# A decoder step on one core: feed-forward without marking products, the last pair's products apart, the last tile added in its bank, first weights on another queue, a planner with new costs

## The chip, the cores and the metric

The kernel runs on one core of one Trainium2 chip. The core has five engines with a queue of instructions each: PE (matrix products into PSUM, whose 2 KB rows are called banks here), ACT, DVE and POOL (elementwise), and SP, which issues most DMA transfers. ACT and POOL issue some too. The metric is the device time in microseconds (us); lower is better. Times are medians of rounds; one execution is also profiled.

## The reference

One inference step of one decoder layer for a prompt of 512 tokens and a sample group of 8 x 4 tokens, which share all weights; D_MODEL is 1024, D_FF 2816, everything in float32.

```python
h = rmsnorm(x, norm_mix)
z = h @ w_in                       # 8 heads of dilated attention, 4 heads of a gated recurrence (HGRN2)
x = x + concat([att, o]) @ w_out   # both normalised per head
c = rmsnorm(x, norm_cross)         # cross attention over 256 memory rows
x = x + co @ w_co
u = rmsnorm(x, norm_ffn)
ug = u @ w_gate
conv = conv_b + sum(conv_w[j] * up[:, j:j + T] for j in range(CONV_W))   # up: ug behind its state
x = x + (jax.nn.silu(conv) * (u @ w_up)) @ w_down
y = rmsnorm(x, norm_final)
```

Beside y the outputs are the new keys and values, the recurrent states, the memory's keys and values and the last rows ahead of the convolution.

## The kernel before, in words

All 544 tokens lie along the free dimension, features on the 128 partitions: x is 8 tiles of 128 x 544. A product of full precision is made of three passes of a faster type (float32r): each operand is split into a high part (a copy, by ACT) and a low part (a subtraction, by DVE), and high x high, high x low and low x high are added in one PSUM bank (`passes`, line 920). A tile of weights (128 output features, 1024 inputs) is thus 24 products for each of two cuts of the tokens: `CUTS`, 256 and 288 columns, or `HALVES`-like cuts of 272.

*Pairs.* Most of the feed-forward takes two tiles of weights together with Strassen's scheme (Winograd's form): seven block products in place of eight, each of 12 passes with 272 columns (`Pair`, line 2356). The seven are numbered as in the code: 1 is A11 x B11, 2 A12 x B21, 6 S2 x U, 7 S3 x X, 5 S1 x T, 3 S4 x B22, 4 A22 x V, where S and U, X, T, V are sums of blocks. Three banks of a pair hold them: "a" takes 1, 6, 5 and 3 in turn, "d" 2, and "c" 7 and 4. Behind 1, 6 and 5 ACT copies bank "a" out (`keep`, line 2422): behind 1 into bank "d", to which product 2 then adds, behind 6 and 5 into an SBUF tile `kept`. Behind 7 DVE reads bank "c" before 4 adds to it. In the loop at line 2493 the products of a pair and of the one before it alternate in the order 1, 3, 2, 6, 7, 4, 5, where 3 and 4 are those of the pair before; 3 and 4 of the last pair so follow its 5. There are 20 pairs of gate and up tiles, four plain tiles ahead of them (gate 0, up 0, gate 1, up 1: `plain_tile`), and the same scheme again for the down product (`DownPair`, `LastPair`).

*Marking.* A product whose first pass says start replaces what is in the bank; one that does not adds. Bank "d" is filled by ACT and then added to. Ahead of the first such use each bank is written once by a product with start over 272 columns, whose value nobody reads: `mark_banks` (line 2474) does so for the five banks of the pool `PX`, `mark_down` (line 2485) for the two of `PD` and the one of `PDEC`.

*The end.* The last two tiles of the down product (m = 6 and 7) take the tokens in the cuts `LAST_CUTS`: 288 first, then 256 (`last_half`, line 2522). DVE adds the bank to x, ACT squares the sum, PE sums the squares over the partitions, ACT makes the factor `r_final` of the norm (`final`, line 2541), and DVE (11 of 16 pieces) and POOL (5) write y, which SP and ACT store. For m = 7 the second cut is the last product of the kernel.

*The start.* SP loads, in this order, part of x tile 0, the weights wf of tile 0 in two parts, the rest of x tile 0, and then x and wf by turns for tiles 1 to 7; ACT's queue loads the first eight columns of gains (`vec`), by which x is multiplied when it is split. ACT and DVE split each tile; DVE adds the squares of x into `acc_mix`, from which PE makes the first norm's sums (`psr_mix`).

*What sets the order.* The class `Tape` (line 270) records every call of an engine instead of making it, with an estimated length, and `order` (line 456) then plays a list schedule with these estimates, in which the dense products ("main") keep the order in which they were written and all other work is put where its due time (`begin`) and the free engines allow; the calls are then made in that order. Its constants at line 278 say, among others, how far ahead of its due time work may begin (`LEAD`), how much is taken as a reserve (`SLACK`, `MARGIN`), how long small PE products are saved up for a joint burst between dense ones (`BURST`, `PATIENCE`), and what a change of PE's mode costs (`SWITCH`). `fits` (line 538) asks whether a buffer of the kind that a step needs is free; it counts the free ones. The lengths of instructions stand in `take` (line 674).

Every recorded call carries the line of the recorder itself in the profile, L713 before and L724 after the change; instructions are so told apart by their tiles.

## Time and profile before

| | us |
|---|---|
| median of 3 rounds | 799.51 (799.26 to 799.98) |
| profiled execution | 798.79 |
| its span, from the first to the last instruction | 797.0 |
| PE busy in the span | 784.1 |
| DVE, ACT, POOL busy | 673.9, 480.1, 206.6 |

The stages follow each other: the first norm and the first three tiles of w_in up to about 25 us, the mixers (attention and recurrence) with the memory's keys and values up to 306, w_out up to 355, cross attention up to 428, the feed-forward with its down product up to 786, and then the last norm and the stores of y. A line of the timeline has the start in us, the length in us, engine, source line, operation, output <- inputs, the form, a count, and in brackets the idle time of the engine before it with what ended it. PE's instructions overlap, so their pace is read from start to start. "SPq" and "ACTq" are the queues' own instructions, such as the issue of a DMA.

### The profile page before, as it was taken

Reading aid. Unit: us, or ns where it says so; the run is one execution under the profiler, and the core shown is the slowest. Engines: PE = TensorE matmul, PEld = TensorE weight load, DVE = VectorE, ACT = ScalarE, POOL = GpSimd, SP = SyncE. Lnnn points to the kernel's source line nnn. Section 1 sums busy time; section 2 is a strip of 40 time slices with the busy share of each in tenths; the row PEclk is TensorE's granted clock in tenths of the full one; section 3 lists DMA queues with packets and bytes.
Section 4 is the critical chain, followed back from the end, with each engine's and each line's share of the span. In section 5 each row is a group of like instructions: output and inputs, shape, how many; then the busy total and the mean of one; then the engine's idle time right before and its main releaser. Section 6 shows DMA issues by size and latency. Waiting matters only on the chain.

```text
span 797.0 us, 19226 instructions
## 1 busy us (share of the span) xinstructions
PE 784.1 (98%) x7440; PEld 742.0 (93%) x7440; DVE 673.9 (85%) x1507; ACT 480.1 (60%) x1040; POOL 206.6 (26%) x284
## 2 busy tenths in 40 slices
PE   9999999999999999999999999999999999999995
PEld 9998878887898989999999999999999999999994
DVE  6889888578978886674888999999999998989963
ACT  8724468826558545553685767656665766567642
POOL 1131200030211110231234337423532433232023
PEclk9999999999999999999999999999999999999998
DMA  9753897799652364441754467877968877786103
GB/s 306 260 147 103 282 322 223 261 353 305 207 203 80 109 215 153 132 147 52 255 165 119 83 173 177 188 177 199 186 159 192 204 160 186 185 240 158 52 1 112
DMA packets 107419, 144.12 MB, mean 181 GB/s; under 512 B 7360, under 2 KB 73920, under 8 KB 107328
## 3 DMA queue, kind: packets, MB, share of 16 engines
q1 hardware_dynamic: 91728, 124.01, 48.3%
q0 software_dynamic: 14880, 18.36, 14.5%
q8 instruction: 58, 0.95, 0.5%
q10 hardware_dynamic: 720, 0.53, 0.2%
q14 instruction: 33, 0.27, 0.1%
HBM read 134.80 MB, written 8.07 MB: 179 GB/s over the span
## 4 chain that ended last, share of the span: by engine, by line
PE 97%; ACT 1%; DVE 1%; issue 0%; DVEq 0%; ACTq 0%
PE ps_ag L713 7%; PE ps_au L713 7%; PE ps_wo L713 6%; PE ps_aw L713 5%; PE ps_cu L713 4%; PE ps_cg L713 4%; PE ps_q L713 3%; PE ps_co L713 3%; PE ps_cq L713 3%; PE ps_first L713 3%; PE ps_dz L713 3%; PE ps_az L713 3%; PE ps_hv L713 2%; PE ps_cw L713 2%; PE ps_dg L713 2%; PE ps_ck L713 2%
## 5 line engine op out<-in xcount | busy, mean ns | idle before, releaser
L713 DVE TENSOR_TENSOR wl<-wr,wh 128x512 fp32r<-128x512 f32 x98 | 69.5, 733 | 3.3 <-ACT wh L713 3.2
L713 ACT CAST wh<-wr 128x512 fp32r<-128x512 f32 x98 | 56.3, 618 | 11.9 <-DMA wr<-in_w_in 6.1
L713 POOL TENSOR_TENSOR hG<-hG,hf 128x256 f32<-128x256 f32 (+1 forms) x28 | 25.1, 897 | 134.4 <-DVE hf L713 79.5
L713 POOL COPY last<-ug 128x2 f32<-128x2 f32 (+1 forms) x44 | 31.9, 788 | 59.0 <-DVE ug L713 56.4
L713 DVE SCALAR_TENSOR_TENSOR cv<-ug,vec,cv 128x560 f32<-128x560 f32 x44 | 35.2, 800 | 1.6 <-ACT cv L713 1.1
L684 POOL DMA_DIRECT2D S13w<-in_w_down x12 | 12.2, 1013 | 61.3 <-DVE ug L713 8.3
L713 POOL TENSOR_TENSOR acc_cx<-acc_cx,sq_cx 128x256 f32<-128x256 f32 (+1 forms) x14 | 12.6, 904 | 56.7 <-PE ps_wo L713 30.7
L713 ACT COPY keptg<-ps_ag 128x272 f32<-128x272 f32 x20 | 7.7, 386 | 28.9 <-PE ps_ag L713 28.9
L713 ACT ACTIVATE cv<-ug,vec 128x560 f32<-128x560 f32 x22 | 18.9, 858 | 4.7 <-POOL ug L713 3.5
L713 DVE TENSOR_TENSOR xr<-xr,ps_wo 128x256 f32<-128x256 f32 (+1 forms) x16 | 6.8, 436 | 15.1 <-PE ps_wo L713 15.1
L713 ACT ACTIVATE cv<-cv 128x560 f32<-128x560 f32 x22 | 14.8, 671 | 7.7 <-DVE cv L713 7.5
L713 PE MATMUL ps_co<-coh,wh 128*128 128x256 f32 (+1 forms) x64 | 19.0, 297 | 0.0
L713 POOL TENSOR_TENSOR acc_final<-acc_final,sq_final 128x256 f32<-128x256 f32 (+1 forms) x10 | 8.2, 834 | 40.2 <-ACT sq_final L713 40.1
L713 PE MATMUL ps_co<-coh,wl 128*128 128x256 f32 (+1 forms) x64 | 18.4, 288 | 0.0
L713 PE MATMUL ps_co<-col,wh 128*128 128x256 f32 (+1 forms) x64 | 18.4, 288 | 0.0
L713 POOL COPY ug<-conv_state 128x16 f32<-128x16 f32 x22 | 17.9, 992 | 0.0
L713 ACT ACTIVATE P<-P,mx 128x128 f32<-128x128 f32 (+3 forms) x32 | 17.6, 553 | 0.2
L713 ACT COPY hsm<-psA 64x128 f32<-64x128 f32 x4 | 1.0, 258 | 26.0 <-PE psA L713 17.7
L713 POOL MEMSET hG<- 128x544 f32 x4 | 2.2, 550 | 56.0 <-PE psr_att L713 45.9
L713 DVE TENSOR_TENSOR xr<-xr,ps_aw 128x272 f32<-128x272 f32 x36 | 15.6, 433 | 0.8 <-PE ps_aw L713 0.5
L713 DVE TENSOR_TENSOR hf<-hf 128x256 f32<-128x256 f32 (+1 forms) x28 | 12.2, 435 | 4.8 <-POOL hG L713 4.5
L713 PE MATMUL psd<-st,qbd_win 128*32 128x224 f32 x256 | 16.0, 358 | 0.0
(3348 smaller groups left out, 3812.7 us busy)
## 6 DMA issues: line engine op xcount, KB each, us to landing
st<-in_kwT SPq DMA_DIRECT2D x32, 448.0 KB, 5.6
st<-in_vw SPq DMA_DIRECT2D x28, 512.0 KB, 5.5
wr<-in_w_in SPq DMA_DIRECT2D x25, 512.0 KB, 6.6
wrg<-in_w_gate SPq DMA_DIRECT2D x10, 512.0 KB, 5.7
wru<-in_w_up SPq DMA_DIRECT2D x10, 512.0 KB, 4.8
st<-in_mkT SPq DMA_DIRECT2D x8, 512.0 KB, 5.4
wr<-in_w_out SPq DMA_DIRECT2D x8, 512.0 KB, 3.7
S13w<-in_w_down SPq DMA_DIRECT2D x24, 128.0 KB, 3.2
```

What stands on the lines that cost most here:

```text
L684: return tape.put(engine, lambda: call(*args, **kw), outs, ins, 0.1, 0.3, size)
L713: return tape.put(engine, lambda: call(*args, **kw), outs, ins, length, lag, size, port, codes, work, mode)
```

## The change

1. *Marking.* `mark_banks` and `mark_down` are gone. In the first three pairs (`MARKED = 3`) product 1 is followed by one product with start into bank "d". The plain tiles gate 1 and up 1 are cut at 272 + 272 columns (`HALVES`), so that their banks are written over 272 columns.
2. *Last pair.* In the last pair the order of the loop is 1, 3, 2, 6, 4, 5, 7.
3. *Last tile.* For m = 7, second cut, ACT copies x into the bank ahead of the products, which then add to it; ACT squares the bank itself, and DVE copies the bank to x in place of the add.
4. *First weights.* The two parts of wf of tile 0 are issued on ACT's queue, ahead of the load of its function table; the first gains are issued on SP, second, behind the first part of x.
5. *Recorder.* Several constants and lengths have other values, and `fits` counts a freed buffer (of all kinds but "a") as free from the time at which the buffer that was given back first, in the order of the program, is free. This moves instructions on all engines.

```diff
+HALVES = ((0, N // 2), (N // 2, N // 2))
+MARKED = 3
...
-    ROUNDS, EVEN = 2, 1.013
+    ROUNDS, EVEN = 2, 1.029
     BLOCK, AHEAD_OF, FETCH = 256, 63, 4.3
-    SWITCH, NEAR = 0.14, 3.9
-    SPELL, ACTIVE, IDLE, COLD = 3.4, 0.45, 0.45, 2.0
-    BURST, PATIENCE, SLACK, LEAD, MARGIN = 1.75, 3.7, 16.5, 15.95, 4.95
+    SWITCH, NEAR = 0.16, 4.85
+    SPELL, ACTIVE, IDLE, COLD = 3.4, 0.47, 0.45, 2.0
+    BURST, PATIENCE, SLACK, LEAD, MARGIN = 1.75, 8.45, 15.3, 14.5, 4.65
...
         def fits(s):
             want = needs(s)
-            return all(room[k] >= v for k, v in want.items()) and ("a" not in want or leaves_room(s, want["a"]))
+            return all(room[k] >= v if k == "a" else len(give[k]) >= v and max(give[k][:v]) <= now + 1e-9
+                       for k, v in want.items()) and ("a" not in want or leaves_room(s, want["a"]))
...
-    nc.scalar.dma_start(vec[:, :KT], vecs[:, :KT])
...
     with tape.as_written():
+        for c0, c1 in ((0, 128), (128, 384)):
+            nc.scalar.dma_start(wf[0][:, c0:c1], w_first[0][:, c0:c1])
         nc.scalar.preload_act_table_set(LN_SET)
         x_load(0, 0, 256)
-        for c0, c1 in ((0, 128), (128, 384)):
-            nc.sync.dma_start(wf[0][:, c0:c1], w_first[0][:, c0:c1])
+        nc.sync.dma_start(vec[:, :KT], vecs[:, :KT])
         x_load(0, 256, N)
...
-        for cut in CUTS:
+        for cut in CUTS if i < ffn_w + 2 else HALVES:
...
+                if first and bank == "a" and self.mark:
+                    self.s["d"] = PX(f"ps_d{self.name}")
+                    nc.tensor.matmul(self.s["d"][:, :HT], w[0][0], xs[0][0], start=True, stop=True)
...
-    def mark_banks():
-
-
-        for i in range(5):
-            nc.tensor.matmul(PX(f"ps_mark{i}")[:, :HT], ux[0][0][:, :128], ux[0][0][:, :HT], start=True, stop=True)
...
-    def mark_down():
-
-        for ps in (PD("ps_mark_a"), PD("ps_mark_d"), PDEC("ps_mark_c")):
-            nc.tensor.matmul(ps[:, :HT], b_side("B11")[0][0][:, :128], b_side("B11")[0][0], start=True, stop=True)
...
-        for i in (1, 3, 2, 6, 7, 4, 5):
+        for i in (1, 3, 2, 6, 4, 5, 7) if unit is units[-1] else (1, 3, 2, 6, 7, 4, 5):
...
         ps = PF(f"ps_dz{m}_{c}")
+        if m == KT - 1:
+            nc.scalar.copy(ps[:, :n], x[m][:, cut])
         with tape.main():
-            passes(ps, held[m], hs, n0, n, range(k))
-        add_to(m)(ps, n0, n)
+            passes(ps, held[m], hs, n0, n, range(k), copied=m == KT - 1)
         if m < KT - 1:
+            add_to(m)(ps, n0, n)
             ssq3.add(x[m][:, cut], n0, nc.vector if m == KT - 2 else None)
         else:
-            nc.scalar.activation(last_sq[:, cut], x[m][:, cut], AF.Square)
+            nc.scalar.activation(last_sq[:, cut], ps[:, :n], AF.Square)
+            nc.vector.tensor_copy(x[m][:, cut], ps[:, :n])
```

The lengths that `take` gives to instructions change by small amounts too (a transpose 0.1 in place of 0.11, an addition on POOL 0.0021 an element in place of 0.0026, and so on), and two groups of small products have a fixed length added.

Three places in the built order, in which names carry buffer numbers and rows of equal form have the letters h and l for high and low parts.

PE, end of the last pair (u20). T x S1 is product 5, B22 x S4 product 3, both in bank "a" (ps_au); the last three passes of the one and the first three of the other, before:

```order
L713 MATMUL ps_au_2109<-Th_1394,S1u20h 128x272
L713 MATMUL ps_au_2109<-Tl_1395,S1u20h 128x272
L713 MATMUL ps_au_2109<-Th_1394,S1u20l 128x272
L713 MATMUL ps_au_2109<-B22h_1408,S4u20h 128x272
L713 MATMUL ps_au_2109<-B22l_1409,S4u20h 128x272
L713 MATMUL ps_au_2109<-B22h_1408,S4u20l 128x272
```

and now, behind the same three passes:

```order
L724 MATMUL ps_au_2101<-Th_1389,S1u20h 128x272
L724 MATMUL ps_au_2101<-Tl_1390,S1u20h 128x272
L724 MATMUL ps_au_2101<-Th_1389,S1u20l 128x272
L724 MATMUL ps_cu_2124<-Xh_1378,S3u20h 128x272
L724 MATMUL ps_cu_2124<-Xl_1379,S3u20h 128x272
L724 MATMUL ps_cu_2124<-Xh_1378,S3u20l 128x272
```

The twelve passes of product 7 (X x S3, bank "c", ps_cu) have moved in between; they stood ahead of product 4 of the pair before, which comes earlier by as much. Product 4 of u20 is now two products behind 7, with product 3 between, where there were three between.

PE, the mixers: a pair of tiles of w_in (keys) that is made by the same scheme, products 5 and 3 in bank ps_ak. psd are scores of the sample group. Before:

```order
L713 MATMUL ps_ak_313<-xTh_240,S1h_k_307 128x272
L713 MATMUL ps_ak_313<-xTl_241,S1h_k_307 128x272
L713 MATMUL ps_ak_313<-xTh_240,S1l_k_308 128x272
L713 MATMUL ps_ak_313<-xm4h,S4h_k_309 128x272
L713 MATMUL ps_ak_313<-xm4l,S4h_k_309 128x272
```

and now:

```order
L724 MATMUL ps_ak_313<-xTl_241,S1h_k_307 128x272
L724 MATMUL ps_ak_313<-xTh_240,S1l_k_308 128x272
L724 MATMUL psd_320<-st_319,qbd_win 32x224 x4
L724 MATMUL psd_320<-knew,qbd_win 32x32 x4
L724 MATMUL psd_320<-st_321,qbd_win 32x224 x4
L724 MATMUL ps_ak_313<-xm4h,S4h_k_309 128x272
```

Three of seven rows of psd that stood ahead of product 5 have moved in between.

DVE, the end: the pieces y of the first cut (r_final_2296 before, r_final_2288 now) and of the second. Before:

```order
L713 TENSOR_TENSOR xr_962<-xr_962,ps_dz_1_2302 128x256
L713 SCALAR_TENSOR_TENSOR y_0_2297<-xr_955,vec,r_final_2296 128x288
L713 SCALAR_TENSOR_TENSOR y_0_2298<-xr_957,vec,r_final_2296 128x288
L713 SCALAR_TENSOR_TENSOR y_0_2299<-xr_959,vec,r_final_2296 128x288
L713 SCALAR_TENSOR_TENSOR y_0_2300<-xr_960,vec,r_final_2296 128x288
L713 SCALAR_TENSOR_TENSOR y_0_2301<-xr_962,vec,r_final_2296 128x288
L713 SCALAR_TENSOR_TENSOR y_1_2305<-xr_955,vec,r_final_2304 128x256
```

and now:

```order
L724 COPY xr_962<-ps_dz_1_2294 128x256
L724 SCALAR_TENSOR_TENSOR y_0_2289<-xr_955,vec,r_final_2288 128x288
L724 SCALAR_TENSOR_TENSOR y_0_2290<-xr_957,vec,r_final_2288 128x288
L724 SCALAR_TENSOR_TENSOR y_0_2291<-xr_959,vec,r_final_2288 128x288
L724 SCALAR_TENSOR_TENSOR y_0_2292<-xr_960,vec,r_final_2288 128x288
L724 SCALAR_TENSOR_TENSOR y_0_2293<-xr_962,vec,r_final_2288 128x288
L724 SCALAR_TENSOR_TENSOR y_1_2297<-xr_955,vec,r_final_2296 128x256
```

Nothing has moved here: the copy out of the bank stands where the add stood, ahead of all pieces.

More of the change, by code (lines that the diff above doesn't have):

```diff
@@ L473, in order @@
         takes = sorted(takes.items(), key=lambda t: t[1])
+        give, over = {k: [0.0] * n for k, n in room.items()}, {}
         waiting = {e: [] for e in ("PE", "ACT", "DVE", "POOL", "SP")}
@@ L563, in start @@
                 room[k] -= v
+                if k != "a":
+                    del give[k][:v]
             for n in s.tiles:
@@ L587, in start @@
                 clock[:] = s.est, now
+            gone = []
             for n in s.tiles:
@@ L590, in start @@
                     left[n] -= 1
+                    over[n] = max(over.get(n, 0.0), s.end + s.lag)
                     if not left[n]:
                         ends.pop(n, None)
-                        frees.append((s.end + s.lag, self.kinds[n]))
+                        frees.append((over[n], self.kinds[n]))
+                        gone.append((over[n], self.kinds[n]))
+            for t, k in sorted(gone):
+                give[k].append(t)
             todo -= 1
@@ L692, in take @@
                 else:
-                    least = 0.112 if m == 128 and k == 128 else 0.0105
+                    least = 0.112 if m == 128 and k == 128 else 0.0093
                     length = 2 * max(least, 0.00086 * n * (max(m, 128 - 2 * k) / 128 if m < 128 else 1.0) * (0.59 if k <= 64 else 1.0))
@@ L917, in tile_decoder_step, with passes @@
     stream = Stream()
-    def passes(ps, w, xs, n0, n, order, first=True, last=True):
+    def passes(ps, w, xs, n0, n, order, first=True, last=True, copied=False):
         for at, i in enumerate(order):
@@ L923, in passes @@
             for j, (a, b) in enumerate(((hi, xh), (hi, xl), (lo, xh))):
-                nc.tensor.matmul(ps[:, :n], a, b[:, n0:n0 + n], start=(first and at == 0 and j == 0),
-                                 stop=(last and at == len(order) - 1 and j == 2))
+                nc.tensor.matmul(ps[:, :n], a, b[:, n0:n0 + n], start=(first and not copied and at == 0 and j == 0),
+                                 stop=(last and at == len(order) - 1 and j == 2), skip_group_check=copied)
     def half(w, xs, name, evac, cut, order=None):
@@ L2361, in __init__ @@
             src = w_gate if kind == "g" else w_up
+            self.mark = (kind, j) in PAIRS[:MARKED]
             def load():
@@ L2424, in fn @@
                 if name == "q":
-                    out = self.s["d"] = PX(f"ps_d{self.name}")
+                    out = self.s["d"] if self.mark else PX(f"ps_d{self.name}")
+                    self.s["d"] = out
                 elif name == "z":
@@ L2472, in tile_decoder_step @@
     seq.insert(-1, units[0].q.pop(1))
-    def mark_banks():
-        for i in range(5):
-            nc.tensor.matmul(PX(f"ps_mark{i}")[:, :HT], ux[0][0][:, :128], ux[0][0][:, :HT], start=True, stop=True)
-    later.pe(mark_banks)
     later.pe(lambda: ffn_in.rows(1))
-    seq[1:1] = [later.order.pop(), later.order.pop()]
+    seq.insert(1, later.order.pop())
     before = None
-    def mark_down():
-        for ps in (PD("ps_mark_a"), PD("ps_mark_d"), PDEC("ps_mark_c")):
-            nc.tensor.matmul(ps[:, :HT], b_side("B11")[0][0][:, :128], b_side("B11")[0][0], start=True, stop=True)
-    later.pe(mark_down, tok_low["B11", 0])
-    marks = later.order.pop()
     for u, unit in enumerate(units + [None]):
         q, b = unit.q if unit else {}, before.q if before else {}
-        if u == 1:
-            seq.append(marks)
-        for i in (1, 3, 2, 6, 7, 4, 5):
+        for i in (1, 3, 2, 6, 4, 5, 7) if unit is units[-1] else (1, 3, 2, 6, 7, 4, 5):
             s = b if i in (3, 4) else q
```

12 lines of the change are left out of this document (7 added, 5 removed).

## The prediction

> **What bounds the kernel now.** I read the page first, then the waits of PE, then the windows by stage, then the timeline at each place that the change touches.
>
> ```profile
> span 797.0 us, 19226 instructions
> PE 784.1 (98%) x7440; PEld 742.0 (93%) x7440; DVE 673.9 (85%) x1507; ACT 480.1 (60%) x1040; POOL 206.6 (26%) x284
> PE 97%; ACT 1%; DVE 1%; issue 0%; DVEq 0%; ACTq 0%
> PE ps_first L713 <- DVE zero L713: 1.1, 1, 1.1
> PE ps_au L713 <- ACT keptu L713: 0.9, 1, 0.9
> PE psds L713 <- ACT ho L713: 0.7, 1, 0.7
> PE psr_final L713 <- ACT sq_last L713: 0.5, 1, 0.5
> PE ps_ak L713 <- ACT keptk L713: 0.5, 1, 0.5
> 480.00:580.00 100.00, 99.91 (x797) 99.69 (x796) 95.99 (x206) 66.05 (x140) 48.74 (x64) 1.00 0.83 184
> ```
>
> PE works 784.1 of 797.0 us and is 97% of the chain that ended last, at a granted clock of 1.00 (the figure behind POOL's in a window). The waits add up to 3.7 us. So three things can move the time: PE instructions taken out, these waits, and the two ends, where PE is not alone. Anything saved on other engines is hidden under PE. In the windows the columns are PE, PEld, DVE, ACT, POOL: the feed-forward leaves DVE 4 us of 100 idle, which I keep for the rivals.
>
> **The marking products.** Eight go (five at line 2478, three at 2488) and three come (one in each of the first three pairs).
>
> ```profile
> 432.01 1.01 PE L713 MATMUL ps_mark<-ux0h 128*128 128x272 f32 x5
> 432.86 0.29 PE L713 MATMUL ps_g<-ux0h,wh 128*128 128x288 f32 x1
> 461.62 0.28 PE L713 MATMUL ps_mark_a<-B11h 128*128 128x272 f32 x1
> 461.99 0.29 PE L713 MATMUL ps_au<-B11h,A11u2h 128*128 128x272 f32 x1
> 457.25 1.51 PE ps_ag L713 x12
> ```
>
> Durations here overlap, so the price is from start to start. Three marks fill 461.62 to 461.99, 0.37 us, which is the pace of a product (1.51 / 12 = 0.126). The five fill 0.85 us, 0.22 more than five at that pace: the restart after the norm sums just before them, which the next product will inherit. Net five products: 5 x 0.126 = **-0.63 us**, bounds -0.85 (were nothing inherited) and -0.4 (were the new marks to wait a little for bank "d", which they now take a product earlier). Cutting the tiles g1 and u1 at 272 + 272 in place of 256 + 288 leaves the same 544 columns: 0.
>
> **The last pair's products.** In every pair the fifth product ends with a copy of its bank by ACT, and the third adds to that bank. In the last pair they follow each other.
>
> ```profile
> 725.31 0.28 PE L713 MATMUL ps_au<-Th,S1u20l 128*128 128x272 f32 x1
> 726.48 0.39 PE L713 MATMUL ps_au<-B22h,S4u20h 128*128 128x272 f32 x1 [0.88 <-ACT keptu L713]
> 726.06 0.36 ACT L713 COPY keptu<-ps_au 128x272 f32<-128x272 f32 x1
> 724.41 0.44 DVE L713 TENSOR_TENSOR ug<-ps_cg,keptg 128x272 f32<-128x272 f32 x1
> 724.76 0.68 DVE L713 TENSOR_TENSOR wdlz<-wdz,wdhz 128x512 fp32r<-128x512 f32 x1
> 726.19 0.80 DVE L713 SCALAR_TENSOR_TENSOR cv<-ug,vec,cv 128x560 f32<-128x560 f32 x1
> ```
>
> As the order of PE shows (under the change), the twelve passes of the seventh product now stand between the two, so 1.5 us of work covers the copy. The stall is 726.48 - 725.31 - 0.126 = 1.04 us; the copy was done at 726.42, even late, and the third product is now due 1.51 + 0.13 after 725.31, at 726.95. What is late next: the bank ps_cu. Its fourth product, now with only the third between it and the seventh, must wait until DVE has read it, and ahead of that read DVE has ug<-ps_cg, two low parts of weights and two cv: 0.44 + 2 x 0.68 + 2 x 0.80, and 0.44 for the read, 3.84 us, after ps_cg is ready. PE has 3 x 1.51 = 4.53 us of products in that time. 0.7 us of slack, less some 0.3 to hand over, and cv also waits for ACT. I take 0.1 us of new wait: **-0.94 us**, bounds -1.04 and -0.3.
>
> **The end.** Copying x into the bank ahead of the products and squaring from the bank takes the add from ahead of the square.
>
> ```profile
> 786.46 0.42 DVE L713 TENSOR_TENSOR xr<-xr,ps_dz 128x256 f32<-128x256 f32 x1 [3.11 <-PE ps_dz L713]
> 786.80 4.69 DVE L713 SCALAR_TENSOR_TENSOR y<-xr,vec,r_final 128x288 f32<-128x288 f32 x11
> 783.51 0.42 ACT L713 ACTIVATE r_final<-r_fin 128x288 f32<-128x288 f32 x1
> 786.91 0.42 ACT L713 ACTIVATE sq_last<-xr 128x256 f32<-128x256 f32 x1 [2.51 <-DVE xr L713]
> 788.62 0.39 ACT L713 ACTIVATE r_final<-r_fin 128x256 f32<-128x256 f32 x1
> 787.33 6.18 SPq L684 DMA_DIRECT2D out_yT<-y  x12
> 289.88 0.29 DVE L713 COPY hS<-psU 128x128 f32<-128x128 f32 x1
> 287.58 0.29 DVE L713 TENSOR_TENSOR htm<-htm 128x128 f32<-128x128 f32 x1
> ```
>
> The chain of waits goes through the add and the square, and by it 0.45 us would be saved (786.91 - 786.46). But five of the eleven y belong to the first part of the tokens and have had their r_final since 783.93; they stand behind the add, in order, and DVE runs all eleven without a gap until 791.49, while SP issues its twelve stores without a gap from 787.33 on, 0.51 us each. The second r_final comes at 789.01, when the fifth y is just done.
>
> In DVE's new order the copy out of the bank has the add's place, and a copy out of PSUM took as long as an add of that shape (0.29 and 0.29). So r_final comes 0.45 us earlier and waits for DVE. **0**, bounds -0.45 (the chain) and 0.
>
> **The start.** The weights of tile 0 leave SP's queue for ACT's, the first eight gains the other way.
>
> ```profile
> 1.18 0.90 SPq L684 DMA_DIRECT2D wf<-in_w_first  x2
> 3.06 0.51 ACT L713 ACTIVATE xm0h<-x,vec 128x256 fp32r<-128x256 f32 x1 [0.60 <-DMA vec<-in_vecs]
> 4.11 0.40 ACT L713 CAST wfh<-wf 128x256 fp32r<-128x256 f32 x1 [0.54 <-DMA wf<-in_w_first]
> 8.47 0.51 ACT L713 CAST wfh<-wf 128x384 fp32r<-128x384 f32 x1 [0.48 <-DMA wf<-in_w_first]
> 18.40 3.21 DVE L713 TENSOR_TENSOR acc_mix<-acc_mix,sq_mix 128x544 f32<-128x544 f32 x4
> 21.66 1.19 PE L713 MATMUL psr_mix<-acc_mix,sums 128*128 128x256 f32 x4
> DMA  0000007985989968999999879999999999899999
> ```
>
> psr_mix starts at 21.66 because acc_mix ends at 18.40 + 3.21 = 21.61; ACT, which splits the tiles ahead of DVE, has worked without a gap since the weights that it waited for at 8.47. So the stage ends as much earlier as those land. Two loads less and one more ahead of them on SP is one issue, 0.45 us. The last row is the DMA engines' busy share over the first 12 us, 0.3 us a digit: full from 4.5 us on, with holes before, so an earlier issue finds room. Against it vec is now second on SP and lands perhaps one issue later than now, when xm0h waited for it until 3.06; ACT stood idle for 0.54 up to 4.11 and can recover there. **-0.35 us**, bounds -0.45 and +0.4.
>
> [...]
>
> **The planner.** New costs and the new rule for freed buffers move side products between the dense ones from 22 to 428 us; from 430 on the order of PE is otherwise unchanged.
>
> ```profile
> 91.80 0.39 PE L713 MATMUL ps_ak<-xm4h,S4h_k 128*128 128x272 f32 x1 [0.47 <-ACT keptk L713]
> 91.04 0.29 PE L713 MATMUL ps_ak<-xTh,S1l_k 128*128 128x272 f32 x1
> 295.29 0.66 PE L713 MATMUL psds<-cs,domn 128*128 128x128 f32 x4 [0.67 <-ACT ho L713]
> 452.58 3.18 PE ps_u L713 x24
> 388.42 3.38 PE ps_cq L713 x24
> ```
>
> For ps_ak the fifth and third products of a pair stood together too; now part of the scores psd, which stood a little earlier, is between them. That wait, 91.80 - 91.04 - 0.126 = **-0.63 us**, goes (bounds -0.63 and 0). psds moves ahead of pso, whose copy it waited for: **-0.67** (bounds -0.67 and 0; a full set of banks can make it wait for another). Side products between dense ones now come in 55 groups in place of 58; a group costs about 3.38 - 3.18 = 0.20 us at its edges (24 products of 288 columns behind one, and with none): **-0.6**, bounds 0 and -0.6. Against this, rows put elsewhere will wait somewhere: the three waits above average 0.67 us, and I take one and a quarter of them, **+0.8**, bounds 0 and three, 2.0.
>
> **Sum.** -0.63 - 0.94 + 0 - 0.35 - 0.63 - 0.67 - 0.60 + 0.80 = -3.0 us. The profiled execution took 798.8 us, 0.7 under the median 799.5, so 795.8 as a profile and **796.5** as a median.
>
> **Rivals.** (1) *The planner gives nothing*: as many waits and edges as before, the start eaten by vec; -0.63 - 0.94 = -1.6, 797.9. For it: nearly every side product from 90 to 300 has moved. Against: the two waits have visibly lost their cause. 2 in 10. (2) *The start gives nothing*, the DMA engines and not SP's issues being the limit from the first byte: 796.9. Against it: the holes before 4.5 us. 1 in 10. (3) *All pays*: no new waits, and the tail follows the chain: -3.82 - 0.45, 795.2; 1 in 10. (4) *Slower: DVE cannot feed the feed-forward.* Work off PE may now begin only 14.5 us ahead of its due time, not 15.95; a low part of a weight that misses its product stalls PE, and DVE's 4 idle us of 100 leave little to catch up with. There are 20 pairs; from 0.23 us each it eats 3.0 + 1.6 and is slower; at 0.25, 5 us, 801.5. For it: 95.99 busy. Against: PE waits there once now, and DVE's order in that stretch moves by one or two places. Under 1 in 10. My forecast: 5 in 10.
>
> **Numbers.** 0.2% (1.6 us) is about what a measurement can tell from no change. Faster: forecast, (2), (3) and a little of (1), 0.76; same: the rest of (1), 0.17; slower 0.07. The range goes from below (3), 794.6, to above (1), 799.0.
>
> **What would show it.** Right: no wait of ps_au on keptu, of ps_ak on keptk, of psds on ho; PE's first dense row after the norm sums follows at once; psr_mix at about 21.3; r_final 0.45 us earlier against the last dense product, with DVE's eleven y starting no earlier. Wrong: new rows among PE's waits between 90 and 300 of over 1 us in all, or waits on low parts of weights between 480 and 740; or a span from the last dense product to the end that has shrunk by 0.4.

## The result, and the profile after

| | before | after |
|---|---|---|
| median of four rounds | 799.70 (799.26 to 799.98) | 792.02 (791.72 to 793.45) |
| ratio, 95% interval | | 0.9906 (0.9891 to 0.9920) |
| profiled execution | 798.79 | 791.79 |
| its span | 797.0 | 790.0 |
| PE busy | 784.1 | 778.9 |

The change is faster by 7.7 us. I had forecast 3.0 (796.5; 794.6 to 799.0). The sign was right; the size was not, and the time lies below the range.

The page of the kernel after: span, busy times, and the chain that ended last; then all rows of PE's waits.

```profile
span 790.0 us, 19226 instructions
PE 778.9 (99%) x7435; PEld 739.8 (94%) x7435; DVE 673.6 (85%) x1507; ACT 484.4 (61%) x1041; POOL 209.4 (27%) x284
PE 89%; DVE 8%; issue 1%; DMA 1%; ACT 0%; SPq 0%; POOL 0%; DVEq 0%; ACTq 0%
PE ps_first L724 <- DVE zero L724: 1.1, 1, 1.1
PE psr_final L724 <- ACT sq_last L724: 0.5, 1, 0.5
PE ps_first L724 <- ACT xm0h L724: 0.3, 1, 0.3
PE ps_aw L724 <- DVE xr L724: 0.2, 1, 0.2
```

The waits of ps_au on keptu, ps_ak on keptk and psds on ho are gone, and two short ones have come. The 8% of DVE in the chain come from the last of them: followed back from ps_aw at 496 us, the chain runs through DVE most of the way from 426 us on. In the second profiled execution of the change, which lacks this wait, PE has 98% of the chain again. But the listed waits fell by only 1.6 us (3.7 to 2.1). PE's *busy* time fell by 5.2, with five products fewer that cost 0.63. Most of the gain is thus inside what the view of waits calls busy.

Where it came from is read from the first products of the stages. Before, psr_mix (the sums of the first norm) began at 21.66 and w_out at 306.74; after:

```profile
21.30 1.08 PE L724 MATMUL psr_mix<-acc_mix,sums 128*128 128x256 f32 x4
301.38 0.28 PE L724 MATMUL ps_wo<-om0h,wh 128*128 128x256 f32 x1
423.06 0.28 PE L724 MATMUL ps_g<-ux0h,wh 128*128 128x256 f32 x1
779.33 0.59 PE L724 MATMUL psr_final<-acc_final,sums 128*128 128x256 f32 x2
```

and before:

```profile
306.74 0.28 PE L713 MATMUL ps_wo<-om0h,wh 128*128 128x256 f32 x1
428.41 0.28 PE L713 MATMUL ps_g<-ux0h,wh 128*128 128x256 f32 x1
786.26 0.59 PE L713 MATMUL psr_final<-acc_final,sums 128*128 128x256 f32 x2
```

| stretch | before | after | difference | my terms |
|---|---|---|---|---|
| to psr_mix | 21.66 | 21.30 | -0.36 | -0.35 |
| mixers, psr_mix to w_out | 285.08 | 280.08 | **-5.00** | -1.10 |
| w_out, cross attention | 121.67 | 121.68 | 0 | 0 |
| feed-forward and down product, to the last norm sums | 357.85 | 356.27 | -1.58 | -1.57 |
| last norm sums to the end | 10.73 | 10.65 | -0.08 | 0 |

The whole miss is in the mixers. That the feed-forward agrees with my terms to 0.01 is in part luck: in the second profiled execution of the change this stretch takes 355.71, 2.14 less than before, most of the difference being the wait of ps_aw. The same two stretches of the mixers in the windows (PE, PEld, DVE, ACT, POOL, each busy time with its count; then PEclk, DMA share and GB/s), before and after:

```profile
21.60:306.70 285.10, 283.66 (x3415) 248.02 (x3415) 238.21 (x623) 163.95 (x363) 42.53 (x50) 1.00 0.66 216
```

```profile
21.30:301.40 280.10, 280.07 (x3417) 247.40 (x3416) 240.25 (x624) 165.95 (x364) 41.82 (x50) 1.00 0.67 219
```

PE was idle for only 1.4 us in this stage before. With the same products it is now busy for 3.6 us less.

*The last pair after.* Product 5 ends, 7 follows at once, then 3:

```profile
717.82 0.29 PE L724 MATMUL ps_au<-Th,S1u20l 128*128 128x272 f32 x1
717.94 0.29 PE L724 MATMUL ps_cu<-Xh,S3u20h 128*128 128x272 f32 x1
719.45 0.28 PE L724 MATMUL ps_au<-B22h,S4u20h 128*128 128x272 f32 x1
720.39 0.43 DVE L724 TENSOR_TENSOR up<-ps_cu,keptu 128x272 f32<-128x272 f32 x1
720.94 0.33 PE L724 MATMUL ps_cu<-Vh,A22u20h 128*128 128x272 f32 x1
```

No gap but the pace (0.12) stands ahead of 7 and of 3. DVE has read ps_cu at 720.82, just before product 4 needs it. My slack was thus rightly small.

*The two waits of the mixers after:*

```profile
89.23 0.29 PE L724 MATMUL ps_ak<-xTh,S1l_k 128*128 128x272 f32 x1
89.45 0.58 PE L724 MATMUL psd<-st,qbd_win 128*32 128x224 f32 x8
90.40 0.40 PE L724 MATMUL ps_ak<-xm4h,S4h_k 128*128 128x272 f32 x1
284.87 1.04 PE L724 MATMUL psds<-cs,domn 128*128 128x128 f32 x8
```

*The end after:*

```profile
779.53 0.42 DVE L724 COPY xr<-ps_dz 128x256 f32<-128x256 f32 x1 [3.10 <-PE ps_dz L724]
779.87 4.66 DVE L724 SCALAR_TENSOR_TENSOR y<-xr,vec,r_final 128x288 f32<-128x288 f32 x11
779.99 0.38 ACT L724 ACTIVATE sq_last<-ps_dz 128x256 f32<-128x256 f32 x1 [2.51 <-DVE xr L724]
780.40 6.11 SPq L695 DMA_DIRECT2D out_yT<-y  x12
781.67 0.39 ACT L724 ACTIVATE r_final<-r_fin 128x256 f32<-128x256 f32 x1
```

The square still waits for DVE. It starts 0.46 behind DVE's *copy*, as it started 0.45 behind the *add* before: ACT's idle time of 2.51 ends with an instruction of DVE that only reads the same bank.

### The profile page after: what moved, and what is told of

Its sections match the earlier page's. It is cut to its first block, busy times and chain, and to the rows that moved or that the text cites. A ratio compares the mean times of both kernels' runs of the same rounds, so it can differ in the third digit from the quotient of the medians.

```text
span 790.0 us, 19226 instructions
## 1 busy us (share of the span) xinstructions
PE 778.9 (99%) x7435; PEld 739.8 (94%) x7435; DVE 673.6 (85%) x1507; ACT 484.4 (61%) x1041; POOL 209.4 (27%) x284
## 4 chain that ended last, share of the span: by engine, by line
PE 89%; DVE 8%; issue 1%; DMA 1%; ACT 0%; SPq 0%; POOL 0%; DVEq 0%; ACTq 0%
PE ps_au L724 6%; PE ps_wo L724 6%; PE ps_ag L724 6%; PE ps_aw L724 4%; PE ps_cu L724 3%; PE ps_q L724 3%; PE ps_co L724 3%; PE ps_cq L724 3%; PE ps_cg L724 3%; PE ps_dz L724 3%; PE ps_az L724 3%; PE ps_hv L724 2%; PE ps_cw L724 2%; PE ps_first L724 2%; PE ps_ck L724 2%; PE psd L724 2%
## 5 line engine op out<-in xcount | busy, mean ns | idle before, releaser
L724 POOL COPY last<-ug 128x2 f32<-128x2 f32 (+1 forms) x44 | 34.5, 859 | 63.4 <-DVE ug L724 60.3
L724 POOL COPY ug<-conv_state 128x16 f32<-128x16 f32 x22 | 19.9, 982 | 0.0
L724 DVE CUSTOM_DVE_ANT_0 P<-psS,bias 128x128 f32<-128x128 f32 (+3 forms) x32 | 14.2, 485 | 1.5 <-PE psS L724 1.5
L724 PE MATMUL psdo<-st,dpt 128*32 128x256 f32 x224 | 15.3, 384 | 0.0
```

The lines of the kernel that those rows point to most:

```text
L724: return tape.put(engine, lambda: call(*args, **kw), outs, ins, length, lag, size, port, codes, work, mode)
```

## The experiments

All edits are against the kernel before or the change, as said. The start of psr_mix, the mixers (psr_mix to w_out) and the end (from the last norm sums) are those of each run's profiled execution. The runs were made on five chips; each ratio is to the kernel before on the same chip, where its median was 799.2 to 800.1. Eight of the profiled executions have the same order of PE in the mixers, row for row, and no wait of psT (below); they take 280.08 to 280.65 there, so a difference of 0.6 between single executions says little.

| run | median | ratio to before, 95% | psr_mix | mixers | end |
|---|---|---|---|---|---|
| old planner, four edits | 800.18 | 1.0002 (0.9991 to 1.0013) | 21.76 | 284.76 | 10.64 |
| new planner alone | 795.47 | 0.9944 (0.9932 to 0.9956) | 22.25 | 280.65 | 10.72 |
| constants alone | 796.19 | 0.9951 (0.9936 to 0.9966) | 22.18 | 281.58 | 10.65 |
| lengths alone | 796.47 | 0.9956 (0.9944 to 0.9969) | 21.85 | 282.24 | 10.63 |
| six lengths of calls | 799.11 | 1.0004 (0.9991 to 1.0016) | 21.84 | 284.15 | 10.64 |
| two fixed additions | 797.99 | 0.9983 (0.9974 to 0.9993) | 21.54 | 283.54 | 10.64 |
| rule alone | 798.78 | 0.9991 (0.9979 to 1.0003) | 21.72 | 284.49 | 10.65 |
| constants and lengths, no rule | 795.32 | 0.9945 (0.9930 to 0.9960) | 22.15 | 280.58 | 10.73 |
| the change again | 792.30 | 0.9916 (0.9902 to 0.9929) | 21.94 | 280.12 | 10.67 |
| change, old loads | 792.96 | 0.9919 (0.9906 to 0.9931) | 22.35 | 280.46 | 10.65 |
| change, old last pair | 794.76 | 0.9934 (0.9920 to 0.9947) | 22.10 | 281.41 | 10.64 |
| change, old marks | 793.98 | 0.9926 (0.9912 to 0.9941) | 23.49 | 280.17 | 10.56 |
| change, copy on ACT | 793.07 | 0.9916 (0.9902 to 0.9929) | 23.26 | 281.62 | 9.94 |
| and a store moved | 791.39 | 0.9905 (0.9888 to 0.9921) | 22.00 | 280.47 | 9.95 |
| and POOL done early | **790.18** | 0.9882 (0.9867 to 0.9896) | 23.33 | 280.64 | 8.66 |
| and old loads | 790.98 | 0.9888 (0.9868 to 0.9908) | 21.86 | 280.58 | 8.65 |
| or new loads, gap filled | 791.51 | 0.9892 (0.9873 to 0.9911) | 22.04 | 282.52 | 8.64 |

### Which edits carry it: the written ones or the planner

The change with the planner of before:

```diff
-    BURST, PATIENCE, SLACK, LEAD, MARGIN = 1.75, 8.45, 15.3, 14.5, 4.65
+    BURST, PATIENCE, SLACK, LEAD, MARGIN = 1.75, 3.7, 16.5, 15.95, 4.95
...
```

> The four written edits (marks, last pair, last tile, first weights) with the planner of before: all constants, lengths and the rule for free buffers as they were. PE's order differs from before in the edited places alone, and by eight scores psd that move one place. Theory A (the planner makes the gain between 75 and 312 us, the written edits only their own terms): 0.6 + 1.1 + 0.35 + 0 = about 2.1 us less than before, 797.5; the same products of the mixers stand 0.2 to 0.5 us earlier than before, and the waits of ps_ak on keptk and of psds on ho are still there. Theory B (the earlier start carries the mixers: tiles of w_in split earlier, so that side work comes in better order): about 5 us or more less, 794.5 or lower, and the mixers end over 3 us earlier.

Neither came: no gain at all. In the mixers it is as theory A had it (284.76, both waits still there). But the marks and the last pair brought their terms and lost them again to waits that neither kernel has. PE's waits in this run:

```profile
PE ps_ez L715 <- DVE xr L715: 1.0, 1, 1.0
PE ps_dw L715 <- ACT ps_dw L715: 0.8, 1, 0.8
PE psds L715 <- ACT ho L715: 0.7, 1, 0.7
PE psr_final L715 <- ACT sq_last L715: 0.5, 1, 0.5
PE ps_ak L715 <- ACT keptk L715: 0.5, 1, 0.5
```

The first two are waits of the down product on DVE and ACT in the feed-forward, where DVE is 96% busy. The written edits make the list be laid anew there too.

The planner alone, on the kernel before:

```diff
+    BURST, PATIENCE, SLACK, LEAD, MARGIN = 1.75, 8.45, 15.3, 14.5, 4.65
...
+            give[k].append(t)
```

> Before with nothing but the planner of the change (constants, lengths, rule for free buffers); PE's order in the mixers is that of the change, row for row. Theory A: 5 us less than before, 794.5 to 795, nearly all of it between 75 and 312 us; ps_au still waits 0.9 for keptu, the marks still stand, psr_mix still starts at 21.66. Theory B: under 2 us less, 797.5 or more. My prediction's term for the planner alone was -0.63 - 0.67 - 0.60 + 0.80 = -1.1, 798.4.

This is theory A, though half a us above its range: 4.5 us less (0.9944), the mixers 4.4 shorter. The planner carries the miss. The terms do not add up: 0 for the four edits, 4.5 for the planner, 7 to 7.7 together.

### Constants, lengths, and the rule for buffers

Constants alone; lengths alone; six lengths of calls without the two fixed additions; the two additions alone:

```diff
+    BURST, PATIENCE, SLACK, LEAD, MARGIN = 1.75, 8.45, 15.3, 14.5, 4.65
```

```diff
+                    n, length = 128, 0.1
...
+                tape.cur.length += 0.14
```

> Before with the new constants alone (BURST, PATIENCE, SLACK, LEAD and their neighbours), old lengths and old rule for buffers. The small products come in 54 groups in place of 58, with 168 changes of shape in place of 174. If the gain goes with the number of changes of shape and groups, this has all of it: 4 to 5 us less than before. If it goes with the three waits and with the particular rows that stand side by side, it may be anything from 0 to -5, and the waits of PE tell which.

> Before with the new lengths alone, old constants and old rule for buffers: 54 groups, 168 changes of shape, as many as with the constants, but in another order. If the gain goes with the number of changes: 4 to 5 us less than before, and within 0.8 us of the run with the constants. If it goes with the waits and the particular neighbours: the two differ by over 1 us, and the one that keeps the waits of ps_ak and psds has 1.3 us less of the gain.

> Before with six of the new lengths (transposes, small products, ACT, POOL), without the fixed additions to the two groups of small products. 56 groups of small products in place of 58, but 174 changes of shape, as many as before. The stage from the first norm sums (psr_mix) to the first product of w_out took 285.1 us before, 280.1 in the change, 281.6 with the constants alone and 282.2 with all lengths alone (54 groups, 168 changes each). If the gain goes with the number of groups: -0.8 each, 283.5. If it goes with the number of changes of shape: 0, 285. If it goes with particular waits (ps_ak on keptk, psds on ho, the second of two scores psS on its bank): what those rows say, 0.6 to 0.8 for each that is gone.

> Before with the two fixed additions alone (0.14 and 0.22 to two groups of small products). 58 groups as before, but 169 changes of shape in place of 174. Groups: 0, the stage at 285. Changes of shape: -0.5 each, 282.5. Particular waits: what those rows say, 0.6 to 0.8 for each that is gone.

With 54 groups and 168 changes of shape each, the first two runs gave -3.5 and -2.8 in the mixers, within 0.8 of each other, which spoke for the number of changes. The other two were to decide, and by them neither number carries it. The six lengths (56 groups, 174 changes) gave -0.9 and the additions (58, 169) -1.5; both counting theories missed both. Particular waits fit better, but not fully. The six lengths lose psds' wait, but bring two of pst_hk, 1.5 on hk and 0.5 on hAT; without these 2.0 they would stand at -2.9, with as many changes as before. The additions keep both old waits, ps_ak's and psds', and still gain 1.5, of which 0.4 in the scores psS (11.45 to 11.02, see below); the rest is not accounted for.

The rule alone, and constants and lengths without the rule:

```diff
-            return all(room[k] >= v for k, v in want.items()) and ("a" not in want or leaves_room(s, want["a"]))
+            return all(room[k] >= v if k == "a" else len(give[k]) >= v and max(give[k][:v]) <= now + 1e-9
...
```

> Before with the new rule for freed buffers alone, old constants and lengths: 57 groups of small products, 169 changes of shape. Before, at 190.93 and at 230.54, the first of two scores psS starts alone, and the second, which runs beside it elsewhere, waits 0.55 and 0.36 for its bank (until ACT has copied hAT out of psL). Theory A (the rule keeps a step from being put where its bank is believed free and is not): both waits go, 0.9 less, and the stage from psr_mix to w_out, 285.1 before, comes to 283.5 with the five changes of shape fewer. Theory B (where things stand is settled by constants and lengths, and these waits go or stay by chance of the order): anything between 282.5 and 285.5, with the waits of ps_ak and psds still there.

> Before with the new constants and lengths, but the old rule for freed buffers. PE's rows stand in the same order as with the whole planner (run with nothing but the planner: stage 280.65, no waits of ps_ak, psds or of a second psS). Theory B above: the same stage within 0.4, and about 795.5 in all. Theory A: 0.9 or more longer.

Theory B in the main: with constants and lengths, the mixers take 280.58 without the rule and 280.65 with it, PE's order being the same. The rule alone takes 0.6 off, no more than executions of one order differ, and the median is the same as before within its interval. Of the waits that theory B wanted still there ps_ak's is; psds' is gone, and psr_att waits 0.5 for ho in its place. The rule leaves one of the two waits that it was to prevent: the first of two scores psS still starts alone at 190.98 and the two still take 1.67.

### What lies inside PE's busy time

Two scores psS of 64 rows, two passes each, ran beside each other in the change and took 1.13 us. Before, around 190.93, they did not and took 1.68; PE, PEld and ACT in that stretch:

```profile
190.93 1.68 PE L713 MATMUL psS<-k,q 64*128 64x512 f32 x4
191.07 0.36 ACT L713 COPY hAT<-psL 64x256 f32<-64x256 f32 x1
191.49 0.29 PEld L713 LDWEIGHTS psS<-k,q 64*128 64x128 f32 x2 [0.26 <-ACT hAT L713]
```

and the same two scores in the change:

```profile
186.72 1.13 PE L724 MATMUL psS<-k,q 64*128 64x512 f32 x4
```

The second score waited for its bank until ACT had copied hAT out of psL. PE was busy with the first alone, so no row of its waits shows it; a row of PEld does. All 64 psS of this kind took 11.45 us from start to start before and 10.64 after.

The price of the shapes by itself, on the kernel before, with a strip ahead of the marks whose values nobody reads:

```diff
+        dense(24)
+        probe(4)            # 4 x 4 of 32 columns, 4 x 2 of 64 rows, 4 of 128 x 128
+        dense(12)
+        for _ in range(4):
+            probe(1)        # the same 28 products, in turns
+        dense(12)
+        for _ in range(4):
+            probe(1)
+            dense(3)
+        dense(24)
```

> Before, with the five marks preceded by a strip of products whose values nobody reads, on banks that the marks write over afterwards: 24 dense; a group of small ones (four times four of 32 columns, four times two of 64 rows, four of 128 x 128), 12 dense; the same small ones in turns, four times (4, 2, 1) in one group, 12 dense; the same again in four groups with 3 dense behind each; 24 dense. The second strip has 9 changes of shape more than the first, the third 3 groups more than the second. Theory A (each change of shape costs, within a group too): the second takes 9 x 0.15 to 0.25 = 1.3 to 2.2 us more than the first, the third some 0.6 more than the second. Theory B (only the edges against dense products cost, 0.20 a group, as my prediction counted): the second as long as the first, within 0.3, the third 0.6 more.

The three strips in the windows (PE busy and its count; a small product counts twice, since it is made in two passes):

```profile
434.99:439.49 4.50, 4.50 (x58) 1.00 0.47 168
441.16:447.26 6.10, 6.10 (x58) 1.00 0.00 0
448.93:456.15 7.22, 7.22 (x67) 1.00 0.43 142
```

The same 28 products take 4.50 us by kinds and 6.10 in turns: 1.60 for nine changes, 0.18 each, all of it under "busy". That is theory A. Its second half fell with theory B: the third strip, less its nine dense products between the groups (9 x 0.126), is 6.09, as long as the second. Going over a few dense products costs no more than going to the next small shape at once. What is paid in these strips is the change of shape, 0.18, not the group.

### The end

Three runs on the change: the copy on ACT behind its square; then also the store of the last y on SP; then also all eight y of the last cut on DVE.

```diff
-            nc.vector.tensor_copy(x[m][:, cut], ps[:, :n])
+            nc.scalar.copy(x[m][:, cut], ps[:, :n])
```

> The change with one line altered: the copy of the last bank to x is made by ACT behind its square, not by DVE. In the change's trace the square starts 0.46 behind DVE's copy of the same bank, as it started behind the add before, and ACT's instruction waits for DVE. Now the square waits for PE alone, and DVE has nothing ahead of the five y of the first cut, whose factor is there 3 us before the last product. Theory A (the end hangs on DVE's and SP's instructions in order, as my term of 0 had it): the y start about 2.5 us earlier, SP's twelve stores with them, and the whole ends 2 to 3 us earlier than the change, 789 to 790. Theory B (the end hangs on the chain product, square, factor, y): 0.45 less, 791.6. Theory C (the landing of the last stores or POOL's part sets the end): no difference.

```diff
-            (nc.scalar if c and m % 2 else nc.sync).dma_start(yT[128 * m:128 * m + 128, cut], out)
+            (nc.scalar if c and m in (1, 3, 5) else nc.sync).dma_start(yT[128 * m:128 * m + 128, cut], out)
```

> The change with the copy of the last bank on ACT behind its square, as one run before, and the store of the last y (m = 7) moved from ACT's queue to SP's. In that run the end came 9.94 us after the last norm sums began, against 10.65 in the change, and ACT's fourth store, issued last, was behind SP's last by 1.3 us. If the end hangs on the last store issued: 9.1 us from there to the end, 1.5 us less than the change, 790.5 to 791 as a median; if on the landing of stores that wait for each other: 9.9.

```diff
-    ON_POOL = (1, 3, 6), (1, 5)
+    ON_POOL = (1, 3, 6), ()
```

> The change with the copy of the last bank on ACT, the last store on SP, and all eight y of the last cut on DVE, none on POOL. In four profiled executions POOL's last instruction, a DRAIN, took 6.40 us, from the start of its last two y on, and in the two with the copy on ACT the end came 0.8 behind that DRAIN, SP being done 1.4 earlier in the second. Theory A (the end hangs on POOL's DRAIN there): now it starts some 4.5 us earlier and is out of the way; DVE's eight y take 0.8 more, the end comes 9.2 us after the last norm sums began, against 9.95 with POOL and 10.65 in the change. Theory B (the DRAIN waits for something that ends late anyway, such as the last stores): 9.9 or more, with the DRAIN longer.

In the first, the square starts 0.20 behind the last norm sums of acc_final, no more 0.66, and the five y of the first cut run 2.3 us ahead of these sums. From the last norm sums to the end it takes 9.94, 0.7 less than the change. None of my three theories gave that: not 2 to 3 (A), not exactly 0.45 (B), not 0 (C). The median of that run is no better. In its profiled execution the start and the mixers were late, by 1.3 and 1.5 us against the change again (below); of the other four only the whole times are known, 791.20 to 793.24. Its lines at the end:

```profile
780.01 2.22 DVE L724 SCALAR_TENSOR_TENSOR y<-xr,vec,r_final 128x288 f32<-128x288 f32 x5 [0.61 <-ACT r_final L724]
782.30 0.59 PE L724 MATMUL psr_final<-acc_final,sums 128*128 128x256 f32 x2
782.50 0.38 ACT L724 ACTIVATE sq_last<-ps_dz 128x256 f32<-128x256 f32 x1 [2.05 <-PE ps_dz L724]
```

Moving a store gave nothing more (9.95). The third run shows why: 8.66, with DVE's part 0.8 longer.

```profile
783.70 3.22 DVE L724 SCALAR_TENSOR_TENSOR y<-xr,vec,r_final 128x256 f32<-128x256 f32 x8 [2.44 <-ACT r_final L724]
784.61 1.91 ACTq L695 DMA_DIRECT2D out_yT<-y  x3
```

POOL's queue ends with a DRAIN, which the views leave out. In the trace's records it ended 4.95 us after POOL's last y had ended in the kernel before (790.95 and 795.90), in the change (783.99 and 788.94) and here (781.90 and 786.86). Before and in the change SP was done 0.3 us after it, so both ended together. With the end of SP moved forward, the DRAIN was next (in the first two runs SP was done 1.1 and 1.3 us ahead of it); with POOL's last y moved forward, it is out of the way. This version, 790.18, has the lowest median of all: 0.9882 (0.9867 to 0.9896) of before, against 0.9906 and 0.9916 for the change in its two runs; the interval of the first of these (0.9891 to 0.9920) still touches it.

### The last pair and the marks taken back

```diff
-        for i in (1, 3, 2, 6, 4, 5, 7) if unit is units[-1] else (1, 3, 2, 6, 7, 4, 5):
+        for i in (1, 3, 2, 6, 7, 4, 5):
```

> The change with the old order 1, 3, 2, 6, 7, 4, 5 in the last pair too. If the terms add up: the wait of ps_au on keptu is back with 0.9, and 1.0 to 1.1 us more than the change, 793.1. If order and edits hang together: anything else, with new waits in PE's rows.

The wait is back, 1.1 in the rows and 1.24 from start to start (721.68 to 723.05, less the pace). The median is 2.5 above the change's second run, not 1.1. In the profiled execution the rest is a wait of psT in the mixers, described below (0.7 from start to start), 0.4 at one product of ps_hq there, and 0.7 in the feed-forward ahead of the pair, most of it in two places. Two of its five executions took 793.0, as if the terms added up.

```diff
+            nc.tensor.matmul(PX(f"ps_mark{i}")[:, :HT], ux[0][0][:, :128], ux[0][0][:, :HT], start=True, stop=True)
...
```

> The change with the marking products of before (five and three, tiles g1 and u1 at 256 + 288). By my prediction 0.63 more than the change, by the shift along its trace 0.8 (0.55 between the first product of the feed-forward and its first pair, 0.25 between there and the down product): 792.9. If marks and order hang together, a new wait of 0.8 to 1.0 in the feed-forward as in the run with the old planner.

The marks' own price is 0.76 between the first product of the feed-forward and the first of its down products (66.61 us against 65.85 in the change again). With them comes a wait of ps_co on xr ahead of the feed-forward, which the new planner alone has too, and which the new marks remove: w_out and cross attention take 122.39 against 121.67. So the second theory holds in part, with a wait in another place than I had said.

### The start taken back, and its gap filled

The change again as the yardstick of its chip, and with the old loads:

> The change once more, so that the three runs beside it have it on their own chip: 791.5 to 792.5.

```diff
-        for c0, c1 in ((0, 128), (128, 384)):
-            nc.scalar.dma_start(wf[0][:, c0:c1], w_first[0][:, c0:c1])
...
+            nc.sync.dma_start(wf[0][:, c0:c1], w_first[0][:, c0:c1])
```

> The change without its fourth edit: weights of tile 0 on SP's queue and the first gains on ACT's, as before. If the terms add up: psr_mix 0.36 later and 0.4 us more than the change, 792.4. If the edits and the planner's order hang together (each edit lets the list be laid anew, and its waits with it): a difference of 1 us or more, with new rows among PE's waits. If the landing of the first loads differs from execution to execution by as much as the edit moves them: psr_mix anywhere from 21.3 to 22.2.

792.96 and 792.30, with intervals that cover each other. The third theory is borne out by all runs together. In the eleven profiled executions with the old loads psr_mix begins at 21.54 to 22.35, mean 21.94. In the eight with the new loads (the one with the gap filled, below, not counted) it begins at 21.30 to 23.49, mean 22.40. The forecast -0.36 showed up in the one pair of profiles by luck. What did come earlier is acc_mix, whose end was to carry psr_mix along: it ends at 21.50 in the mean with the new loads, at 21.85 with the old ones. In ten of the eleven with the old loads psr_mix follows it by 0.05 to 0.06. In all eight with the new ones it comes 0.21 to 2.15 later than that end, directly behind PE's own products (0.13 behind the last). PE's first product of x waits for ACT's first split, and ACT for the gains: this product starts at 4.12 to 4.31 with the new loads, at 3.64 to 3.77 in ten of the eleven with the old. In the change ACT's first split, the end of acc_mix (17.72 + 3.21 = 20.93) and PE's last product ahead of psr_mix read:

```profile
3.72 0.51 ACT L724 ACTIVATE xm0h<-x,vec 128x256 fp32r<-128x256 f32 x1 [0.78 <-DMA vec<-in_vecs]
17.72 3.21 DVE L724 TENSOR_TENSOR acc_mix<-acc_mix,sq_mix 128x544 f32<-128x544 f32 x4
21.17 0.29 PE L724 MATMUL ps_first<-xm6h,wfl 128*128 128x288 f32 x1
```

In three of the eight, PE's first products stay at half their pace for longer. The windows of the change, and of the run with the copy on ACT:

```profile
3.00:6.00 3.00, 2.71 (x19) 2.41 (x19) 1.57 (x5) 1.54 (x4) 0.00 (x0) 1.00 0.95 273
6.00:9.00 3.00, 2.91 (x24) 2.72 (x23) 2.61 (x5) 2.90 (x6) 0.00 (x0) 1.00 1.03 362
```

```profile
3.00:6.00 3.00, 2.69 (x13) 2.40 (x13) 1.25 (x4) 1.22 (x3) 0.00 (x0) 1.00 0.88 247
6.00:9.00 3.00, 3.00 (x15) 3.00 (x15) 2.46 (x5) 2.76 (x6) 0.00 (x0) 1.00 1.04 386
```

Both are busy, and the granted clock reads 1.00 in both, but 24 products against 15 fit into the second 3 us. The new loads bring the gains later, and PE's step from the twelfth pass over zeros to its next product is 0.55 to 0.74 in all eight; with the old loads it is 0.07 to 0.20, and 0.55 once. The three late executions have 0.70, 0.73 and 0.74; the change itself, with 0.71, was not late. Two runs on the best version asked whether that gap is the cause: old loads again, and new loads with two more products of zeros.

```diff
             warm_up(WARM)
+            kept = tape.cur.length, tape.cur.codes, tape.cur.work
+            warm_up(2)
+            tape.cur.length, tape.cur.codes, tape.cur.work = kept
```

> The run with POOL done early, but with the first weights and gains loaded as before the change. In the nine profiled executions with the old loads psr_mix began at 21.54 to 22.35, in the eight with the new ones five times at 21.30 to 22.10 and three times at 23.26 to 23.49, and in these three PE's first products stayed at 0.21 to 0.24 until 9.4 to 9.8, where the others come to 0.13 by 4.4 to 7.4. Between the twelfth product of zeros (3.56) and the next PE stands idle for 0.60 to 0.74 with the new loads (once 0.55), 0.08 to 0.55 with the old ones. Theory A (the longer gap lets PE stay slow for longer in some executions): no psr_mix beyond 22.4, and as a median 0 to 0.5 less than the run with POOL done early, 789.7 to 790.2. Theory B (the new loads bring the 0.36 that I forecast): 0.4 more, 790.6.

> The run with POOL done early, with the new loads, and two more products of zeros behind the first six (four passes, 0.85 us), so that PE is busy until the first split tile is there; their length is not told to the planner, so that everything else stands in the same order. Theory A: the gap of 0.7 goes, no psr_mix beyond 22.2, 789.6 to 790.2. Theory B (the gap has nothing to do with it): psr_mix at 23.3 in about a third of the executions, the same median as without, 790.2.

Neither has a late start (21.86 and 22.04), as theory A has it. But that is one profiled execution each, and the medians, 790.98 and 791.51, are not below 790.18; theory A wanted at most 790.2. They come from another chip, and by the ratios (0.9888 and 0.9892 against 0.9882) the three intervals cover each other. Open: whether the gap causes the late starts. The last run was also delayed by 1.9 us in the mixers, in part by the wait of psT.

## Why the prediction was right or wrong, point by point

**The bound.** Right that PE bounds the kernel, wrong in what I drew from it: that only PE instructions, listed waits and the two ends can move the time. That left PE's busy time as a fixed price, and it fell by 3.6 us in the mixers alone with the same products.

**The marks**, -0.63: about -0.76, within its bounds.

**The last pair**, -0.94: -1.1 along the two traces, just beyond the bound of -1.04, since the product behind the wait took 0.23 to the next (726.48 to 726.71) in place of 0.12. The wait that I put on ps_cu (0.1) did not come.

**The planner**, -0.63 - 0.67 - 0.60 + 0.80 = -1.1: this step failed; it measured -5.0 in the change and -4.4 with the planner alone. Its first three terms were too small in all, and the fourth did not come. From start to start, against the median of the same form, the profiled pair gives:

- ps_ak's wait -0.64 and psds' -0.84, as I had them within 0.2;
- a wait of ps_ck behind ps_ak, 0.29, and 0.20 in smaller ones, which I had not listed;
- edges between dense and small products -0.82, where I had -0.60;
- scores that ran alone -0.81, which I had not seen;
- the other small products among themselves -0.89. The number of changes of shape among them does not explain it: in this stage PE's order has 57 before and 56 after. How the gain is split between this item and the edges also depends on what is called small: with the norm sums in float32r counted as dense, the edges take -1.9 and this item gives +0.4. Only the two together, -1.5 to -1.7, are firm, and no run separates them;
- about -0.5 that I cannot assign;
- new waits: none in the mixers of this execution, where I had +0.80. Four other executions with the new order have one, that of psT, with 0.3 to 1.1.

What a careful reading would have found ahead of time are the scores: psS took 1.68 for four in a row that elsewhere takes 1.1, and PEld's row names what it waited for. The range failed by the same step: its lower end allowed the planner -1.9 and nothing beyond. That edits and planner would *not* add up (0 and 4.5 against 7.7) I did not consider; the written edits pay with the new constants and lengths, under which the two waits of the run with the old planner do not come; why they do not was not tested.

**The start**, -0.35: confirmed by the profiled pair and refuted by the rest; over all executions the edit brings nothing, and in three of the eight with it psr_mix came over 1 us later. The step that failed is that the stage ends when acc_mix ends. acc_mix did come 0.35 earlier in the mean, but PE, which began some 0.5 later behind the late gains, ended the stage with its own products. My second rival had its result right; its reason is not borne out, since acc_mix did end earlier in the mean: the runs agree with its 0, but do not show full DMA engines to be the cause.

**The end**, 0: right in its number (-0.08), wrong in its mechanism. I wrote that r_final comes 0.45 earlier and then waits for DVE. It did not come earlier at all, since the square waited for DVE's copy. The number was luck. And behind DVE and SP stood POOL's DRAIN.

**Rivals.** "The planner gives nothing" got it the wrong way round: the planner gives most. "All pays" had its condition met in the profiled execution, no new waits in the mixers, and was still 3 us too high, since it too left most of PE's busy time as it was. "DVE cannot feed the feed-forward" did not happen, but the run with the old planner shows its mechanism, with 0.8 and 1.0 in two waits of the down product.

## What to carry to other kernels

Busy time of PE is not a price list: compare the same products from start to start, and read the waits of its weight loads, before taking PE's busy time as fixed. When an order is laid by a scheduler, price an edit together with the order that it brings, and expect its own term back only if the new order has no new waits. At the end of a kernel, look for the last instruction of every queue, a DRAIN included, before shortening the chain of arithmetic.

## What the runs showed of the hardware that I had not expected

- A change of shape between small products cost 0.18 us on PE in the strips, whether or not a few dense products stood between; nine changes took 1.60 of 6.10 us.
- PE's first products change from 0.21 to 0.24 from start to start to about half of that (0.11 to 0.13), at different times for the same order: of the eight executions with the new loads, five came to 0.13 by 4.4 to 7.4 us, and three stayed at 0.21 to 0.24 until 9.4 to 9.8. In five of the eight, the three late ones among them, all windows from 0 to 24 us show the granted clock as 1.00. What sets the moment is not shown.
- POOL's closing DRAIN ended 4.95 us after POOL's last y had ended, in all three traces above. With the last two y on DVE in place of POOL the end came 8.66 us behind the start of the last norm sums, against 9.95.
- The new order hands DVE's PT a buffer of the state hst, whose store must have landed. The two stores took 6.3 us (median) in the change and 8.3 in the run with the copy on ACT, whose rows are below; there DVE waited, and PE's psT behind it. It stands in four runs on the change in all (stores of 8.0 to 8.6 us, 1.6 to 2.4 on DVE, 0.3 to 1.1 on PE), and not in the kernel before.

```profile
DVE PT L724 <- DMA out_ss_out<-hst: 2.1, 1, 2.1
```

```profile
PE psT L724 <- DVE PT L724: 0.8, 1, 0.8
```
